# The order of an encoder kernel's engines, found on a simulated timeline instead of the plain model

## The chip, the core and the metric

The kernel runs on one core of one Trainium2 chip. The metric is the device time of one execution in microseconds (us). A core has five engines that each work through their own list of instructions in order and wait for one another by semaphores: PE (TensorE, matmuls; its weight loads are shown apart as PEld), DVE (VectorE), ACT (ScalarE), POOL (GpSimd) and SP (SyncE, which here only issues DMAs). A profile is one execution taken by the hardware profiler.

## The reference

A two-layer encoder over 512 tokens of width 1024. Each layer projects the normalised input, runs five mixers side by side on parts of the projection, gates their outputs with gates computed from the input, sums them, and closes with an output matmul and a layer norm:

```python
h = layer_norm(x, ln_in_g, ln_in_b)
for l in range(DEPTH):
    p = jnp.einsum('bsd,dc->bsc', h, w_in[l])
    pa, pb, pc, pd, pm = split_last(p, mixer_sizes)
    o_a = mixer_dilated(pa, table_a)
    o_b = mixer_rwkv(pb, ...)
    o_c = mixer_axial_gqa(pc, ...)
    o_d = mixer_diff(pd, ...)
    o_m = mixer_memory(pm, mem, w_mem_kv[l])
    y = gated_merge(h, (o_a, o_b, o_c, o_d, o_m), w_branch[l], w_gate[l], b_gate[l])
    out = jnp.einsum('bsd,de->bse', y, w_out[l])
    h = layer_norm(alpha * h + out, ln_g[l], ln_b[l])
```

Four mixers are attentions over 512 or 256 keys (A dilated, C grouped-query, D differential, M memory). The fifth, B, is a recurrence over the tokens in both directions, eight heads. `gated_merge` is, per mixer, `sigmoid(h @ w_gate) * (o @ w_branch)`.

## The kernel before, in words

**The work.** All activations stay on the core; weights stream in from DRAM in blocks of 128x512 (`load_w`, L125, issued by SP into two buffers per channel, `wrawr` and `wrawf`). A matmul at nearly full fp32 precision is made of three fast ones: `split_w` turns each weight block into a high part (ACT, L135) and a low part (DVE, L136), and `gemm3_steps` issues high x high, high x low and low x high (L149, L150, L151), each 128x512.

**The stages of a layer.** Attention comes first (`att`): for A, C, D and M in turn it projects q, k, v (PSUM tile `pg`), scores (`psc`, L444), softmax on DVE and ACT, transposes (`pt`, L470) and multiplies by v (`po`, L479, L489). For A, D and M `k_stack` copies k to the other half of the partitions by POOL's DMAs (L435, L437). Then the recurrence (`rw`): eight units, one for each pair of heads and direction. `early` prepares a unit (L812 to L941, with the score-like matmuls at L881), `late` solves it: 31 dependent steps of two DVE instructions (L963 and L965), the block inversion on PE (L981, L988), then L1009, L1024, L1035, and a chain of eight states in which PE (L1042), ACT (L1044) and DVE (L1045) take turns. `finish` (L1066 to L1091) normalises a pair of heads. Last comes the out stage: the merge of branch B, the output matmul, the layer norm.

**The filler.** The merge of the other four branches is traced as a generator, `fill`, that is pulled a few matmuls at a time between the steps of C, of M and of the recurrence, and drained after it. Its matmuls go to one PSUM tile of their own, `pf`, so that PE has something to do where the stages have not; in this text they are called filler. There are 1104 of them in a layer, always 128x512: for each of four branches and eight output blocks, 24 for the gate and 6 or 12 for the branch. To each such block belong two or three weight blocks with their splits, an ACT tanh (L380) and two DVE instructions (L388, L390). Branch outputs but A's are spilled to DRAM (`scr_o`) and read back by POOL's DMAs (L366) when four tiles `o` are free.

```python
for _ in recurrence():
    pull(1)
for _ in fl:
    pass
```

**What sets the order.** The kernel's code does not fix an order across the stages. It is traced under the framework's tile context, and every instruction gets its rank from the place where it is traced. When the context closes, a scheduler plays the program against a model of the machine: whenever an engine is free in the model, it gets the instruction of the best rank whose inputs and buffers are ready there. The lists that come out are fixed, one for each engine, and the chip works through them as they stand. So a filler matmul that is traced within the recurrence moves ahead into attention wherever the model shows PE idle there.

## Time and profile before

| | |
|---|---|
| median of 3 runs | 2260.18 us (2258.39 to 2260.19) |
| profiled execution, its own time | 2261.37 us |
| its span | 2259.6 us |
| PE busy | 2186.5 us, 97% |
| DVE busy | 1730.6 us, 77% |
| ACT busy | 1273.2 us, 56% |
| POOL busy | 59.6 us, 3% |
| mean granted TensorE clock | 0.999 of full speed |

Busy time is the union of an engine's instructions. The ends of matmuls are modelled and matmuls overlap, so a PE that shows as busy need not run at its peak. Around the span lie 1.8 us of the execution's own time.

### The profile page before, as it was taken

How to read it: one execution, taken by the hardware profiler on the slowest of the kernel's cores; microseconds unless marked ns; L12 is line 12 of the kernel's file. 1: busy time of each engine (PE TensorE's matmuls, PEld its weight loads, DVE VectorE, ACT ScalarE, POOL GpSimd, SP SyncE). 2: the span in 40 equal slices, each digit the busy share in tenths (PEclk: the TensorE clock that was granted, in tenths of full speed). 3: DMA queues.
4: the chain of work that ended last, by engine and by line, in shares of the span. 5: the costliest groups of instructions: out<-in, count | busy, mean ns of one | idle time of the engine just before them, and what ended most of it. 6: DMA issues, size and time to landing. Idle time of an engine off the chain costs nothing.

```text
span 2259.6 us, 36239 instructions
## 1 busy us (share of the span) xinstructions
PE 2186.5 (97%) x13056; PEld 1678.6 (74%) x13056; DVE 1730.6 (77%) x4236; ACT 1273.2 (56%) x2785; POOL 59.6 (3%) x117
## 2 busy tenths in 40 slices
PE   6999999999999999999999999999999999999998
PEld 5777777777767777777787777777777777777776
DVE  7677887677989797975568778766788979879565
ACT  3565666676665555644326656677675646565440
POOL 0000000100000000000000000001000000000000
PEclk9999999999999999999999999999999999999999
DMA  7732124322222221315333312333313213222261
GB/s 261 222 108 91 56 80 112 113 86 85 75 80 66 86 88 59 102 49 181 117 115 108 98 62 70 97 106 89 112 57 99 71 62 98 72 80 73 84 195 38
DMA packets 111780, 220.49 MB, mean 98 GB/s; under 512 B 13240, under 2 KB 23224, under 8 KB 111216
## 3 DMA queue, kind: packets, MB, share of 16 engines
q1 hardware_dynamic: 101456, 195.09, 27.0%
q0 software_dynamic: 10144, 23.08, 4.0%
q8 instruction: 103, 1.69, 0.3%
q14 instruction: 77, 0.63, 0.1%
HBM read 187.66 MB, written 27.31 MB: 95 GB/s over the span
## 4 chain that ended last, share of the span: by engine, by line
PE 70%; DVE 14%; ACT 8%; DMA 5%; issue 3%; DVEq 0%; POOL 0%; ACTq 0%; SPq 0%
PE pg L150 10%; PE pg L151 10%; PE pg L149 10%; PE pf L149 6%; PE pf L150 5%; PE pf L151 5%; PE psc L444 4%; PE po L489 3%; PE pt L470 3%; DVE W L965 2%; DVE pr L963 2%; DMA wrawr<-in_w_out_dram 1%; DVE wlof L136 1%; PE po L479 1%; DMA wrawf<-in_w_mem_dram 1%
## 5 line engine op out<-in xcount | busy, mean ns | idle before, releaser
L149 PE MATMUL pg<-hT,whir 128*128 128x512 f32 (+1 forms) x912 | 364.0, 399 | 3.2 <-DVE kl L436 1.4
L150 PE MATMUL pg<-hT,whir 128*128 128x512 f32 (+1 forms) x912 | 365.4, 401 | 0.5 <-DVE hT L176 0.5
L151 PE MATMUL pg<-hT,wlor 128*128 128x512 f32 (+1 forms) x912 | 363.8, 399 | 2.1 <-DVE wlor L136 2.1
L136 DVE TENSOR_TENSOR wlor<-wrawr,whir 128x512 fp32r<-128x512 f32 x240 | 163.9, 688 | 114.8 <-ACT whir L135 104.9
L135 ACT CAST whir<-wrawr 128x512 fp32r<-128x512 f32 x240 | 147.7, 618 | 175.1 <-PE pg L150 116.7
L135 ACT CAST whif<-wrawf 128x512 fp32r<-128x512 f32 (+1 forms) x272 | 164.4, 605 | 135.4 <-PE pf L150 77.9
L149 PE MATMUL pf<-hT,whif 128*128 128x512 f32 x512 | 220.8, 431 | 3.4 <-DVE gt L388 2.8
L136 DVE TENSOR_TENSOR wlof<-wrawf,whif 128x512 fp32r<-128x512 f32 (+1 forms) x272 | 181.4, 669 | 49.2 <-ACT whif L135 43.2
L150 PE MATMUL pf<-hT,whif 128*128 128x512 f32 x512 | 206.7, 404 | 0.0
L151 PE MATMUL pf<-hT,wlof 128*128 128x512 f32 x512 | 205.2, 401 | 0.0
L149 PEld LDWEIGHTS pg<-hT,whir 128*128 128x128 f32 x912 | 172.0, 189 | 40.6 <-issue 3.0
L151 PEld LDWEIGHTS pg<-hT,wlor 128*128 128x128 f32 x912 | 171.9, 188 | 40.0 <-DVE wlor L136 4.9
L150 PEld LDWEIGHTS pg<-hT,whir 128*128 128x128 f32 x912 | 171.9, 189 | 37.8 <-issue 3.9
L176 DVE TENSOR_TENSOR pT<-pt,pT 128x512 fp32r<-128x512 f32 x176 | 114.2, 686 | 34.2 <-ACT pT L175 33.1
L175 ACT CAST pT<-pt 128x512 fp32r<-128x512 f32 x176 | 94.7, 589 | 63.0 <-PE pt L470 61.7
L149 PEld LDWEIGHTS pf<-hT,whif 128*128 128x128 f32 x512 | 96.5, 188 | 35.8 <-DVE gt L388 10.2
L470 PE MATMUL pt<-cst,p 128*128 128x128 f32 x704 | 118.6, 273 | 0.5 <-DVE p L461 0.5
L151 PEld LDWEIGHTS pf<-hT,wlof 128*128 128x128 f32 x512 | 96.4, 188 | 22.2 <-issue 1.6
L963 DVE TENSOR_TENSOR pr<-W,U 128x60 f32<-128x60 f32 (+24 forms) x496 | 103.5, 209 | 11.4
L965 DVE TENSOR_TENSOR W<-W,pr 128x60 f32<-128x60 f32 (+24 forms) x496 | 102.9, 208 | 11.0
L470 PEld LDWEIGHTS pt<-cst,p 128*128 128x128 f32 x704 | 89.8, 141 | 28.4 <-DVE p L461 3.6
L150 PEld LDWEIGHTS pf<-hT,whif 128*128 128x128 f32 x512 | 96.8, 189 | 18.8 <-issue 4.3
(326 smaller groups left out, 4809.1 us busy)
## 6 DMA issues: line engine op xcount, KB each, us to landing
wrawr<-in_w_in_dram SPq DMA_DIRECT2D x224, 256.0 KB, 2.8
wrawf<-in_w_gate_dram SPq DMA_DIRECT2D x160, 256.0 KB, 2.8
o<-scr_o POOLq DMA_DIRECT2D x26, 512.0 KB, 4.5
wrawf<-in_w_branch_dram SPq DMA_DIRECT2D x48, 256.0 KB, 2.7
bias<-scr_toe SPq DMA_DIRECT2D x24, 448.0 KB, 3.3
scr_o<-os SPq DMA_DIRECT2D x20, 512.0 KB, 3.7
wrawf<-in_w_in_dram SPq DMA_DIRECT2D x32, 256.0 KB, 3.0
wrawr<-in_w_out_dram SPq DMA_DIRECT2D x32, 256.0 KB, 2.9
```

What stands on the lines that cost most here:

```text
L135: nc.scalar.copy(hi, raw)
L136: tt(lo, raw, f(hi), ALU.subtract)
L149: mm(ps, ah, bh, start=(i == 0), stop=False)
L150: mm(ps, ah, bl, start=False, stop=False)
L151: mm(ps, al, bh, start=False, stop=(i == n - 1))
L175: nc.scalar.copy(hi, src)
L176: tt(lo, src, f(hi), ALU.subtract)
L444: mm(ps[:, :nk], q[:, i, sl], part[:, i if g is None else g, :nk], start=(j == 0), stop=(j == 1))
L470: nc.tensor.transpose(pt[:, qb * 128:(qb + 1) * 128], p4[qb][:, kb * 128:(kb + 1) * 128], ident)
L489: mm(po, vwin(kb), pT[:, b, :], start=(kb == 0 and b == 0), stop=(kb == nkb - 1 and b == 1))
L963: tt(pr, W[:, t8, s:s + 1].to_broadcast([128, nt, n]), U[:, s:s + 1, rsl].to_broadcast([128, nt, n]), ALU.mult)
L965: tt(W[:, t8, rsl], W[:, t8, rsl], pr, ALU.add)
```

## The change

One keyword. The scheduler's machine model is no longer the plain one but the framework's timeline simulation; ranks, buffers and every instruction stay as they were. All five lists are found anew.

```diff
     o = nc.dram_tensor("out_0_dram", (S, DM), F32, kind="ExternalOutput").ap()
-    with tile.TileContext(nc) as tc:
+    with tile.TileContext(nc, schedule_with_timeline_sim=True) as tc:
         encoder_kernel(tc, *[args[k] for k in _INS], o)
```

What that does to the lists is shown at three places of the first layer; the second layer has the same pattern. In the rows, `pf` is a filler matmul, `pg` a projection, `psc<-kh` and `psc<-kc` a score.

PE in attention C, second block of heads, at the third score of its second half. Before:

```order
L149 MATMUL pg<-hT,whir 128x512
L444 MATMUL psc<-kh,q 128x512
L444 MATMUL psc<-kc,q 128x512
L150 MATMUL pg<-hT,whir 128x512
L444 MATMUL psc<-kh,q 128x512
L444 MATMUL psc<-kc,q 128x512
L151 MATMUL pg<-hT,wlor 128x512
```

The same score now:

```order
L149 MATMUL pf<-o,whif 128x512
L444 MATMUL psc<-kh,q 128x512
L444 MATMUL psc<-kc,q 128x512
L150 MATMUL pf<-o,whif 128x512
L151 MATMUL pf<-o,wlof 128x512
L470 MATMUL pt<-cst,p 128x128 x2
L149 MATMUL pf<-o,whif 128x512
L150 MATMUL pf<-o,whif 128x512
L151 MATMUL pf<-o,wlof 128x512
```

Between two scores that had one projection matmul between them there now stand eleven filler matmuls (the next six continue the pattern) and two transposes.

PE in the recurrence, in the chain of states (L1042) of a unit past its middle. Before:

```order
L1042 MATMUL pt<-ST_5175,PE 128x128
L149 MATMUL pf<-o,whif 128x512
L150 MATMUL pf<-o,whif 128x512
L151 MATMUL pf<-o,wlof 128x512
L940 MATMUL psc<-kes,cst 128x512
L149 MATMUL pf<-o,whif 128x512
L150 MATMUL pf<-o,whif 128x512
L151 MATMUL pf<-o,wlof 128x512
L1042 MATMUL pt<-ST_5176,PE 128x128
```

The chain of such a unit now:

```order
L1042 MATMUL pt<-ST_5175,PE 128x128
L1024 MATMUL pt<-OM,WA 64x128 x4
L1042 MATMUL pt<-ST_5176,PE 128x128
L1042 MATMUL pt<-ST_5175,PE 128x128
L1024 MATMUL pt<-OM,WA 64x128 x4
L1035 MATMUL pt<-UV,OM 64x64 x16
L1042 MATMUL pt<-ST_5176,PE 128x128
L881 MATMUL psc<-AR,BK 128x128 x8
L1042 MATMUL pt<-ST_5175,PE 128x128
```

No filler is left between the states; what stands there is the recurrence's own small matmuls.

Counted in PE's lists of the first layer, up to the first L981 (the first solved unit), from there to the last unit's first L981, and behind it: of 1104 filler matmuls 261, 753 and 90 stand there before, and 944, 160 and none now. The 160 come in the first two of the seven intervals between units; five have none. In the second layer the three counts are the same. Other matmuls of 128x512 move too: 54 projections (`pg`) of the first layer now come ahead of its first L981. From the first layer's last unit to the second layer's first, 351 filler matmuls, 1628 `pg` and 519 `psc` stood in the list, and now 944, 1680 and 478; behind the second layer's last unit, 90 filler matmuls and 192 `psc` stood, and now none and 144.

POOL from attention D's first head to its second (a piece of the difference; `kh` and `kl` are the copies of k, `o` a branch output that the filler reads):

```order
 L435 DMA kh<-kh 64x512
 L437 DMA kl<-kl 64x512
+L366 DMA o<-scr_o 128x1024 x2
+L435 DMA kh<-kh 64x512
+L437 DMA kl<-kl 64x512
+L435 DMA kh<-kh 64x512
+L366 DMA o<-scr_o 128x1024
+L437 DMA kl<-kl 64x512
+L366 DMA o<-scr_o 128x1024
 L435 DMA kh<-kh 64x512
 L437 DMA kl<-kl 64x512
```

The read-back of branch C's outputs, which came behind all of attention in POOL's list, now stands among the copies of k for D's heads.

In SP's list all twelve `scr_toe` writes (L270, tables of the position bias) now stand ahead of the ninth weight block (`wrawr` and `wrawf`, L125); before, the first four stood behind the eleventh block and the others between later ones.

## Rows read from the trace of the kernel before

**Rows 1.** The page, engines and slices: busy us, and the granted clock in tenths.

```profile
PE 2186.5 (97%) x13056; PEld 1678.6 (74%) x13056; DVE 1730.6 (77%) x4236; ACT 1273.2 (56%) x2785; POOL 59.6 (3%) x117
PEclk9999999999999999999999999999999999999999
```

**Rows 2.** The page, the chain that ended last, its shares of the span by engine.

```profile
PE 70%; DVE 14%; ACT 8%; DMA 5%; issue 3%; DVEq 0%; POOL 0%; ACTq 0%; SPq 0%
```

**Rows 3.** Five stretches: start:end, length, busy us (x instructions), clock, DMA share, GB/s.

```profile
0.00:610.30 610.30, 581.42 (x2898) 455.52 (x2899) 464.91 (x1064) 371.00 (x774) 23.86 (x48) 1.00 0.38 118
610.30:1000.40 390.10, 378.52 (x2940) 281.42 (x2941) 331.65 (x928) 224.25 (x543) 5.94 (x11) 1.00 0.25 77
1000.40:1708.50 708.10, 698.51 (x3483) 543.82 (x3483) 516.16 (x1155) 404.14 (x833) 22.82 (x45) 1.00 0.32 100
1708.50:2098.50 390.00, 378.46 (x2939) 281.42 (x2939) 331.61 (x928) 224.25 (x543) 5.94 (x11) 1.00 0.25 77
2098.50:2259.60 161.10, 149.57 (x798) 116.38 (x798) 86.26 (x165) 49.52 (x92) 1.08 (x2) 0.98 0.33 108
```

**Rows 4.** The same view, filler alone (tile pf): PE, PEld, DVE, ACT.

```profile
610.30:1000.40 390.10, 216.05 (x753) 132.19 (x753) 14.48 (x22) 15.04 (x22) 1.00 0.25 77
```

**Rows 5.** PE's timeline, a run of projections: start, length; the first and the fifteenth.

```profile
540.08 0.39 PE L150 MATMUL pg<-hT,whir 128*128 128x512 f32 x1
...
543.33 0.39 PE L149 MATMUL pg<-hT,whir 128*128 128x512 f32 x1
```

**Rows 6.** Stretches again: most of attention A to D, and two of the out stage.

```profile
100.00:550.00 450.00, 445.48 (x2117) 346.53 (x2116) 339.37 (x772) 289.50 (x592) 17.59 (x35) 1.00 0.31 95
...
2150.00:2200.00 50.00, 49.04 (x208) 38.43 (x207) 32.45 (x51) 25.55 (x45) 0.00 (x0) 1.00 0.61 194
2200.00:2250.00 50.00, 50.00 (x218) 40.62 (x217) 23.61 (x51) 1.51 (x3) 0.00 (x0) 1.00 0.09 32
```

**Rows 7.** Groups from 610.3 to 1000.4, the filler's DVE instructions: busy, mean ns, idle before.

```profile
L136 DVE TENSOR_TENSOR wlof<-wrawf,whif 128x512 fp32r<-128x512 f32 x60 | 40.9, 684 | 0.8 <-ACT whif L135 0.7
L388 DVE SCALAR_TENSOR_TENSOR gt<-gt,pf 128x512 f32<-128x512 f32 x21 | 14.3, 683 | 1.9 <-PE pf L151 1.6
L390 DVE TENSOR_TENSOR y<-y,gt 128x512 f32<-128x512 f32 x20 | 13.7, 687 | 0.2
```

**Rows 8.** Waits from 610.3 to 1000.4: us in total, times, longest.

```profile
ACT UV L1003 <- PE pt L1035: 19.1, 6, 3.6
ACT ST L1044 <- PE pt L1042: 14.3, 17, 1.6
DVE nkk L783 <- ACT tmp L205: 10.3, 3, 4.6
```

**Rows 9.** The page, DMA issues: KB each, median us from issue to landing.

```profile
o<-scr_o POOLq DMA_DIRECT2D x26, 512.0 KB, 4.5
```

**Rows 10.** Stretches again: the one in which the first tables are written.

```profile
46.00:54.00 8.00, 5.77 (x34) 4.76 (x33) 1.66 (x3) 2.65 (x6) 0.00 (x0) 1.00 1.07 387
```

**Rows 11.** The chain behind the second layer's last unit: start, us; finish's first matmul.

```profile
2125.41 1.07 PE po L1066 x30
```

**Rows 12.** Stretches at the end, where PE has run out of work.

```profile
2250.00:2254.00 4.00, 0.70 (x4) 0.23 (x2) 3.16 (x8) 0.00 (x0) 0.00 (x0) 0.98 0.00 0
2254.00:2257.00 3.00, 0.00 (x0) 0.00 (x0) 2.41 (x9) 0.00 (x0) 0.00 (x0) 0.50 0.05 18
```

## The prediction

> **What bounds the kernel now.** I read the page first, then the chain of waits, then stretches cut where a layer's recurrence solves its first unit and its last (the first L981 of each). The page has PE busy for 97% of the span, at full clock throughout [rows 1], and the chain that ended last runs through PE for 70% of it, through DVE for 14% [rows 2]. Per stretch, with A up to the first layer's first unit, B its recurrence, C from there to the second layer's first unit, D that recurrence, E the rest: A shows PE busy for 581 of 610 us, C for 699 of 708, and DVE for 465 and 516. In B and D PE is busy for 378 of 390 us and DVE for 332 [rows 3]. Of PE's 378 the 753 filler matmuls cover 216 [rows 4]. So the recurrence by itself does not need PE much; DVE is its engine, and the filler is what keeps PE full beside it. Attention needs PE all the time.
>
> How much room is left inside "busy" is read from the spacing of starts. Fifteen 128x512 matmuls in a row start 3.25 us apart from first to last, 0.232 us each, while each shows 0.39 us [rows 5]. A stretch that shows PE busy for 49.04 of 50 us holds 208 matmuls, the next one, at 50.00, holds 218 of the same kind [rows 6]. So even a stretch that shows as full can have some 5% of room, and not much more.
>
> **The change.** The lists show that it moves PE's work from where PE was cover to where PE is the bound. The plain count: 683 filler matmuls more ahead of the first unit (944 against 261), 593 fewer in each recurrence (160 against 753), 593 more in C (944 against 351), 90 fewer in E. I price each at 0.232 us.
>
> *Stretch A.* 683 x 0.232 = 158 us, and the 54 projection matmuls that came along 12.5 us, together 171 us of PE work more. What PE's idle time takes of it: in 100 to 550 us PE shows 4.5 us idle [rows 6], the lower end, and 5% of these 450 us is 22 us, the upper. I take 10 off, between them, since the filler goes in exactly where the new model saw PE waiting, but PE's list can't step aside where the chip waits elsewhere. At the start SP's list has eight of the twelve table writes moved ahead of weights. 512 KB each, 4.2 MB, take 11 us at the 387 GB/s of the stretch that writes the first four [rows 10]; nothing is the lower end, because what is written early needn't be written later, when PE waits for weights as well. I take 5. A: 171 - 10 + 5 = +166 us.
>
> *Stretch C.* 593 x 0.232 = 138 us, 52 projections more 12 us, 41 gate matmuls (`psc`) fewer -9.5 us: +140. Room as in A, 10 us; against it, the last unit of the first layer has lost 90 filler matmuls that ran beside its chain, 21 us, of which I let 6 come back as idle PE. C: 140 - 10 + 6 = +136 us.
>
> *Stretches B and D.* They lose the filler's share. On PE that is 593 x 0.232 = 138 us, on DVE less: the filler's splits, sums and products there take 40.9 + 14.3 + 13.7 = 69 us for 753 matmuls [rows 7], so 593 take 54 us with them. What ends the recurrence is DVE and the exchange between engines, not PE's throughput: DVE is busy for 332 us of 390, idle for 58, and its waits are for ACT and PE in the solving chain (L1003 for L1035 19.1 us, L1044 for L1042 14.3 us, L783 for ACT 10.3 us) [rows 8], which stays as it is. One end: DVE without its idle time, 332 - 54 = 278 us, 112 less than now. The other: no gain, if the chain's latency fills the time. I take DVE's saving with its idle time unchanged: PE answers the chain faster with no filler queued ahead, but DVE has fewer independent instructions between two waits. B and D: -54 us each.
>
> *Stretch E.* 90 filler and 48 gate matmuls fewer, 32 us of PE work. But from the last unit's first L981 (2098.5) to finish's first matmul pass 27 us [rows 11], in which PE's filler was cover and not cause. The 48 gate matmuls, 11 us, do come off, the 90 (21 us) only in part. I take -17, ends -32 and -11.
>
> *The rest.* POOL's read-backs now stand ahead of copies of k that attention D waits for, and wait themselves for the last filler of branch A. In PE's list that filler ends ahead of the second D head's scores in the new order too, so the wait is over when PE gets there; if not, two read-backs of 4.5 us to landing [rows 9] delay one head, 9 us a layer at most. I take nothing. Every instruction is still there, so nothing else is gained.
>
> **Sum**, against the profiled execution's 2261.4 us (the median of the runs is 2260.2, 1.2 less): +166 + 136 - 54 - 54 - 17 = +177, 2438 us. That is 8% slower. Its own range is 2370 to 2505: the room in A and C from 4.5 to 22 us each, the start from 0 to 11, E's ends, and B and D by 25 us each around -54.
>
> **Rivals.**
>
> *The recurrence falls to DVE's time.* Without filler ahead of it in PE's list every answer to DVE comes at once, and DVE's idle time nearly vanishes. For it: the new DVE list weaves the 31 steps of one unit through the states of the unit before. Against it: the idle time is spent on ACT as much as on PE. B and D -105 each, A and C with 22 us of room, E -32: 2261 + 154 + 124 - 210 - 32 = 2297 us.
>
> *The clock falls.* Where PE runs dry, the trace shows what happens: in the 3 us from 2254, after PE's last matmul at 2250, the granted clock is 0.50, the 1.2 GHz level [rows 12]. Five of seven intervals between units have no filler now. PE's other work there is 378 - 216 = 162 us [rows 3, 4] and the 160 filler matmuls that stay 37; twice the 200 us is more than the 336 that I forecast, PE is the bound again, and B and D give nothing back: 2261 + 166 + 136 - 17 = 2546 us. Against it: PE's list still has small matmuls at every step of the chain there. The Trainium skill, page "TensorE: Matmul & The Clock Gate", the closing table "Why this matters for your kernels", speaks against this change: it warns of idle gaps between bursts of matmuls, after which the clock is back at half. By that rule the time is the 2546 us. The trace agrees at the kernel's end alone; the slices before it all show the full clock [rows 1].
>
> *The filler is free in attention.* The one that ends faster. If PE in attention spends a good part of its "busy" time waiting, filler costs nothing there, while the recurrence still gets shorter. PE's weight loads are busy for 999 of the 1318 us of A and C [rows 3], which leaves 24%, 319 us, and the work added is 311. Then only the start and the gains are left: 2261 + 5 - 108 - 17 = 2141 us. It turns to the fast side once A and C absorb some 197 of the 311 us. Against it: the stretch that is full of nothing but 128x512 matmuls shows weight loads at 40.62 of 50 us, 81%, and attention 346.5 of 450, 77% [rows 6], so 81% is full and the room is 5% again. The Trainium skill, page "Perfetto Trace Analysis", section "Identifying the Most-Contended Engine", says that matmul busy time is a poor measure and to judge headroom by the busy share of LDWEIGHTS; read as it stands, with 100% as full, that gives the 2141 us. The trace agrees that matmul busy time hides waits, but not with 100%.
>
> *Nothing comes of it.* The lists do differ at the places where PE is short of time, so an unchanged time needs gains and losses that cancel.
>
> **How the numbers follow.** A difference of 0.2%, 4.5 us, is about what a measurement of this kernel can tell from no change. Forecast 0.64; DVE's floor 0.16; the clock 0.13; free filler 0.05; no difference 0.02. The first three are slower by far over 0.2%: faster 0.05, same 0.02, slower 0.93. The range goes from 2290, which takes in most of the DVE case, to 2530, short of the full clock case: left out are the two small cases, part of the clock's and a little of DVE's.
>
> **What would show it.** In the profile after: A lengthened by some 166 us and C by some 136, with PE busy as now; between the first and the last L981 of a layer some 336 us with DVE at 275 to 280 us busy and PE near half; the filler's last matmul in the third unit. Wrong in size, if that stretch is nearer 285 or 390 us. Wrong in kind, if A and C grow by less than 100 us each.

## The result, and the profile after

The changed kernel takes 2569.84 us (median of 4 runs, 2567.25 to 2571.63), beside 2259.28 us for the kernel before on the same chip: ratio 1.1371, 95% interval 1.1358 to 1.1385. It is slower by 310 us; the forecast was +177 and its range ended at 2530 us. The side was right, the size was not.

The page of the kernel after, engines, granted clock in 40 slices, and the shares of the chain that ended last ([rows 1, 2] before):

```profile
PE 2295.4 (89%) x13056; PEld 1828.0 (71%) x13056; DVE 1766.3 (69%) x4236; ACT 1271.1 (50%) x2779; POOL 61.0 (2%) x117
PEclk9999999999999977776999999999999998675689
PE 71%; DVE 16%; ACT 6%; DMA 4%; issue 3%; SPq 0%; DVEq 0%; ACTq 0%
```

PE, DVE and POOL have as many instructions as before; ACT has six fewer, all of them table loads (2779 against 2785 in [rows 1]). PE's busy time grew by 109 us, but the span by 306: PE waits more than before. And the clock, which showed full throughout, has two valleys.

The same five stretches, cut at the first and the last unit's first L981 of each layer (start:end, length, then PE, PEld, DVE, ACT, POOL busy, clock, DMA share, GB/s); they answer to [rows 3]:

```profile
0.00:809.40 809.40, 754.38 (x3643) 607.39 (x3644) 541.98 (x1171) 427.00 (x865) 29.98 (x58) 0.99 0.37 116
809.40:1165.20 355.80, 283.19 (x2335) 221.57 (x2334) 284.34 (x843) 177.16 (x466) 1.62 (x3) 0.78 0.12 37
1165.20:2058.80 893.60, 848.11 (x4089) 679.10 (x4089) 582.84 (x1240) 451.81 (x908) 27.79 (x53) 0.97 0.32 98
2058.80:2409.80 351.00, 280.73 (x2335) 220.52 (x2335) 283.89 (x843) 174.31 (x464) 1.61 (x3) 0.78 0.12 37
2409.80:2565.20 155.40, 128.96 (x658) 99.39 (x658) 73.29 (x143) 40.77 (x76) 0.00 (x0) 0.85 0.24 83
```

A is 199 us longer (forecast 166), C 185.5 (136). B and D give back 34 and 39 (54 each), E 6 (17). Look at PE's idle time, length less busy: 29 us before and 55 now in A, 10 and 45 in C, 12 and 73 in B. I had expected A and C to use up idle time; they made more of it.

The filler alone (tile pf) in the first two stretches: 944 matmuls ahead of the first unit, and the rest beside the first units, as the lists said (161 and not 160 here, since one lies across the cut).

```profile
0.00:809.40 809.40, 247.57 (x944) 176.15 (x944) 17.80 (x26) 17.80 (x26) 0.99 0.37 116
809.40:1165.20 355.80, 43.26 (x161) 30.17 (x160) 4.10 (x6) 4.11 (x6) 0.78 0.12 37
```

PE's longest waits over the whole span (us in total, times, longest):

```profile
PE pt L981 <- DVE U L977: 48.0, 7, 14.1
PE pt L1042 <- DVE ST L1045: 32.1, 31, 3.6
PE pf L149 <- DVE gt L388: 29.0, 18, 3.6
PE pg L149 <- DVE k L740: 20.4, 2, 10.4
```

Three of the four are the recurrence's: PE waits for a unit to be solved, for a state, for a prepared k. The third is the filler itself, which in a dense row waits for its one PSUM tile. None of this explains why A and C grew by 82 us more than forecast. So the question for the runs is whether the filler's place did it, or the rest of the new order.

### The profile page after: what moved, and what is told of

Read it like the earlier page. It is cut to its first block, busy times and chain, and to the rows that moved or that the text cites. A ratio compares the mean times of both kernels' runs of the same rounds, so it can differ in the third digit from the quotient of the medians.

```text
span 2565.2 us, 36429 instructions
## 1 busy us (share of the span) xinstructions
PE 2295.4 (89%) x13056; PEld 1828.0 (71%) x13056; DVE 1766.3 (69%) x4236; ACT 1271.1 (50%) x2779; POOL 61.0 (2%) x117
## 4 chain that ended last, share of the span: by engine, by line
PE 71%; DVE 16%; ACT 6%; DMA 4%; issue 3%; SPq 0%; DVEq 0%; ACTq 0%
PE pg L149 10%; PE pg L150 10%; PE pg L151 10%; PE pf L149 6%; PE pf L150 6%; PE pf L151 6%; PE psc L444 3%; PE pt L470 3%; PE po L489 3%; DVE pr L963 1%; DVE W L965 1%; PE psc L881 1%; PE pt L1042 1%; DMA wrawr<-in_w_out_dram 1%; PE pt L1035 1%
## 5 line engine op out<-in xcount | busy, mean ns | idle before, releaser
L135 ACT CAST whir<-wrawr 128x512 fp32r<-128x512 f32 x240 | 148.3, 618 | 222.4 <-PE pg L150 158.2
L149 PE MATMUL pf<-hT,whif 128*128 128x512 f32 x512 | 211.3, 413 | 29.2 <-DVE gt L388 29.0
L149 PEld LDWEIGHTS pg<-hT,whir 128*128 128x128 f32 x912 | 177.1, 194 | 70.2 <-issue 26.4
L150 PE MATMUL pf<-hT,whif 128*128 128x512 f32 x512 | 206.0, 402 | 0.0
L150 PEld LDWEIGHTS pg<-hT,whir 128*128 128x128 f32 x912 | 176.9, 194 | 37.9 <-DVE hT L176 0.9
L458 ACT ACTIVATE p<-p,sst 128x512 f32<-128x512 f32 x128 | 92.4, 722 | 51.3 <-DVE sst L452 50.7
L470 PE MATMUL pt<-cst,p 128*128 128x128 f32 x704 | 110.4, 273 | 0.5 <-DVE p L461 0.5
```

Source lines behind the costliest of these rows:

```text
L135: nc.scalar.copy(hi, raw)
L149: mm(ps, ah, bh, start=(i == 0), stop=False)
L150: mm(ps, ah, bl, start=False, stop=False)
L458: act(p, src, AF.Exp, scale=-1.0, bias=st[:, 0:1], accum_out=st[:, 1:2])
L470: nc.tensor.transpose(pt[:, qb * 128:(qb + 1) * 128], p4[qb][:, kb * 128:(kb + 1) * 128], ident)
```

## The experiments

Theory 1: the filler's place is all. Theory 2: the rest of the new order, which I had priced at nothing, costs as much again. A third possibility was that it gains.

### The filler's place and the rest, apart

**hold**: the timeline order, with the filler queued on PE behind the matmul traced just ahead of it.

```diff
-        owed = [0.0]
+        owed, main, seen = [0.0], [], [len(nc.cur_bb.bb.instructions)]
 
         def pull(x):
             owed[0] += x
+            main.extend(i for i in nc.cur_bb.bb.instructions[seen[0]:] if i.engine == mybir.EngineType.PE)
             while owed[0] >= 1:
                 owed[0] -= 1
-                next(fl, None)
+                with tc.issue_after(main[-1 - 0]):
+                    next(fl, None)
+            seen[0] = len(nc.cur_bb.bb.instructions)
```

> The changed kernel (the simulated timeline finds the order), with every filler matmul queued on PE behind the matmul that is traced just ahead of it: 180 filler matmuls ahead of the first unit's first L981, 834 between, 90 behind (before: 261, 753, 90; the change: 944, 160, 0). All else is free to move. Theory 1, the place of the filler alone makes the change slower: within 1.2% of the kernel before, 2235 to 2287 us, the recurrence near 390 us. Theory 2, the rest of the new order (attention's own order, the early table writes, the recurrence's weave) costs as much again as the filler: 2340 us or more. Theory 3, the rest of the new order gains and the filler's place costs more than it shows: under 2230 us.

Measured: 2438.26 us, ratio 1.0803 (1.0779 to 1.0827). With the filler back beside the recurrence 180 us are still lost: theory 2.

**early**: the plain order, with the filler pulled early.

```diff
-                        pull(0.7)
+                        pull(2.95)
...
                         p4.append(p0)
+                        pull(4.5)
...
-                        pull(0.3)
+                        pull(3.7)
...
-            for _ in recurrence():
-                pull(1)
+            for j, _ in enumerate(recurrence()):
+                pull(4 if j < 19 else 0.17)
```

> The kernel before, its scheduler unchanged, with the pulls of the filler made earlier: 2.95 steps per block of attention C, 4.5 per block of D, 3.7 of M, 4 at each of the recurrence's first 19 yields, 0.17 behind them. Filler ahead of the first L981 918, between first and last 186, behind 0; attention C's last score has 273 ahead of it, D's 483, M's 648 (the change: 310, 501, 672). Theory 1 (place alone): 2520 to 2590 us, attention stretches as long as in the change. Theory 2 (the rest of the order costs as well): 2400 to 2470 us, about what I forecast for the move itself. Theory 3: over 2590 us.

Measured: 2416.61 us, ratio 1.0695 (1.0677 to 1.0713), +158 us; again theory 2. Its five stretches:

```profile
0.00:753.90 753.90, 728.92 (x3499) 571.46 (x3499) 525.41 (x1146) 411.52 (x841) 29.21 (x58) 1.00 0.38 120
753.90:1089.40 335.50, 294.11 (x2479) 215.27 (x2479) 286.73 (x868) 195.03 (x493) 1.61 (x3) 0.92 0.14 47
1089.40:1935.80 846.40, 825.82 (x3946) 644.00 (x3947) 563.59 (x1215) 435.42 (x884) 27.21 (x53) 0.97 0.32 100
1935.80:2269.20 333.40, 290.20 (x2477) 211.53 (x2477) 286.65 (x868) 194.77 (x493) 1.61 (x3) 0.93 0.15 48
2269.20:2419.90 150.70, 127.49 (x658) 99.52 (x658) 73.44 (x143) 40.80 (x76) 0.00 (x0) 0.85 0.25 86
```

This is nearly the move that the forecast worked out, 918 filler matmuls ahead of the first unit where the change has 944, and the plain model orders the rest. Against [rows 3] A is +143.6 us for 657 filler matmuls more ahead of the first unit, 0.219 each; C +138.3 for 567 (918 against 351), 0.244 each; B and D are -54.6 and -56.6, with DVE at 287 us busy. Attention took none of the moved filler for nothing: in the second layer C's scores, from first to last, take 140.4 us in place of 93.5 with 189 filler matmuls more among them, and D's 149.5 in place of 112.5 with 180 more.

**bare** and **bare_timeline**: no filler, in the plain order and in the timeline order.

```diff
-        fl = fill()
+        fl = iter(())
...
-                if y[db] is None:
+                if y[db] is None and done is None:
...
-                        tt(gt, y[db], gt, ALU.add)
```

> The kernel before without the filler: the gates and merges of the branches A, C, D and M are left out, so the sum over branches holds B alone. From the stretches: 2261 less filler's place on PE in A (60 us), C (81), E (21) and with some 340 us in each recurrence: about 2000 us. By my price for room in attention (5%) the stretches A and C lose 55 and 75 us. If the filler was free there (rival), A stays at 605 us. The recurrence: 336 us if DVE's work with its idle time sets it; near 350 or more with a granted clock under 0.8 if the lower clock lengthens it; 280 us if DVE alone.

> The changed kernel without the filler (the same work left out). Theory 1 (place alone): within 1.5% of the same cut made from the kernel before. Theory 2 (the rest of the order costs): 60 us or more above it, in the attention stretches. Theory 3: 30 us or more below it.

Measured: 2088.99 us (ratio to the kernel before 0.9251, 0.9235 to 0.9267) and 2255.89 us (0.9990, 0.9979 to 1.0001). The rest of the new order costs 167 us where there is no filler at all. The stretches of bare, then of bare_timeline:

```profile
0.00:598.10 598.10, 543.05 (x2677) 422.27 (x2677) 451.33 (x1042) 361.81 (x756) 23.83 (x48) 0.97 0.35 113
598.10:926.00 327.90, 259.46 (x2196) 190.78 (x2197) 261.31 (x820) 172.32 (x450) 1.63 (x3) 0.79 0.09 30
926.00:1612.10 686.10, 635.99 (x3124) 490.66 (x3125) 485.16 (x1103) 386.19 (x799) 21.74 (x43) 0.95 0.28 90
1612.10:1935.60 323.50, 253.47 (x2195) 186.90 (x2196) 261.10 (x820) 172.18 (x450) 1.63 (x3) 0.81 0.09 30
1935.60:2087.80 152.20, 128.94 (x658) 100.61 (x658) 68.38 (x135) 40.99 (x76) 0.00 (x0) 0.85 0.26 85
```

```profile
0.00:669.20 669.20, 562.20 (x2695) 442.24 (x2695) 458.84 (x1045) 363.35 (x757) 23.75 (x48) 0.93 0.32 101
669.20:1010.00 340.80, 258.70 (x2181) 202.78 (x2181) 268.71 (x816) 167.24 (x446) 1.64 (x3) 0.71 0.09 28
1010.00:1761.50 751.50, 653.33 (x3140) 511.70 (x3140) 494.70 (x1106) 388.32 (x800) 21.92 (x43) 0.92 0.26 82
1761.50:2100.90 339.40, 248.75 (x2181) 194.13 (x2181) 268.42 (x816) 167.22 (x446) 1.63 (x3) 0.75 0.09 28
2100.90:2253.70 152.80, 127.90 (x658) 99.97 (x658) 68.30 (x135) 40.75 (x76) 0.00 (x0) 0.85 0.25 85
```

Nearly the same work in each stretch, and A is 71 us longer, B 13, C 65, D 16, E 1. In hold, which has its filler at about the place of the kernel before (180 matmuls ahead of the first unit, 261 there), the rest can be read a second time. Its A and C, against [rows 3]:

```profile
0.00:685.90 685.90, 597.40 (x2876) 472.08 (x2878) 472.75 (x1065) 376.81 (x778) 23.60 (x48) 0.95 0.32 104
...
1088.50:1865.60 777.10, 711.43 (x3459) 558.94 (x3459) 525.98 (x1155) 409.85 (x836) 22.78 (x45) 0.96 0.28 90
```

Side by side, from the profiled executions:

| | filler's place (early - before) | rest (bare_timeline - bare) | sum | rest again (hold - before) | measured (after - before) | forecast |
|---|---|---|---|---|---|---|
| A | +143.6 | +71.1 | +214.7 | +75.6 | +199.1 | +166 |
| B | -54.6 | +12.9 | -41.7 | +12.5 | -34.3 | -54 |
| C | +138.3 | +65.4 | +203.7 | +69.0 | +185.5 | +136 |
| D | -56.6 | +15.9 | -40.7 | +10.4 | -39.0 | -54 |
| E | -10.4 | +0.6 | -9.8 | +7.1 | -5.7 | -17 |
| all | +160.3 | +165.9 | +326.2 | +174.6 | +305.6 | +177 |

The two measures of the rest agree within 7 us in every stretch, and the filler's place and the rest nearly add up. A and C stay 16 and 18 us under their sums, as if the filler took up some of the idle time that the rest of the order makes there; B is 7 over.

What was expected of bare alone did not come: about 2000 us, with A and C shorter than before by 55 and 75 us. Without their 261 and 351 filler matmuls they are only 12.2 and 22.0 us shorter. So the filler that stood there before cost 0.05 and 0.06 us each, against 0.22 and 0.24 for what early moved in. It had found time that PE had over: 150 of the 261 stand between attention's last score and the first unit, where bare shows PE idle for 22.8 of 104.2 us, and with them this piece takes 100.2 us and leaves 2.7 idle. One caution: leaving work out also finds all lists anew. D's scores, for one, take 123.9 us in bare and 112.5 in the kernel before.

### What in the rest of the order costs

In the second layer, bare against bare_timeline: attention A's scores span 106.1 and 115.5 us, C's 95.3 and 108.4, D's 123.9 and 146.2, and the recurrence 323.5 and 339.4. The scores of A, C and D are 45 of the 65 us by which the stretch C grew. C and D from first to last score, bare:

```profile
1244.70:1340.00 95.30, 92.06 (x448) 69.39 (x448) 86.19 (x197) 61.89 (x134) 2.07 (x4) 1.00 0.21 67
1340.80:1464.70 123.90, 119.23 (x523) 90.33 (x524) 87.48 (x209) 83.22 (x161) 8.15 (x16) 0.99 0.33 99
```

and bare_timeline:

```profile
1351.00:1459.40 108.40, 99.33 (x474) 76.39 (x473) 88.49 (x194) 63.70 (x134) 2.21 (x4) 1.00 0.22 68
1461.70:1607.90 146.20, 130.21 (x556) 99.27 (x555) 95.12 (x223) 88.38 (x170) 7.66 (x15) 0.95 0.29 88
```

In C DVE is busy for 86 of 95 us, almost as full as PE; my view of attention as PE's alone left that out. The new order puts 26 and 33 matmuls more into C and D, and PE, DVE and ACT all idle more there. In D, bare, three of the waits:

```profile
DVE kl L435 <- ACT kh L433: 13.8, 3, 4.7
DVE wlor L136 <- ACT whir L135: 6.8, 7, 2.0
...
ACT whir L135 <- PE pg L150: 5.4, 4, 1.9
```

and bare_timeline:

```profile
DVE wlor L136 <- ACT whir L135: 20.9, 13, 4.3
...
ACT whir L135 <- PE pg L150: 17.8, 9, 4.8
```

DVE's longest wait in bare, for the copies of k, is not among those of bare_timeline; there it waits for the weight blocks. ACT's copy of a weight block waits for the projection matmul that frees its buffer, DVE's split waits for that copy, and the softmax instructions behind the split in DVE's list wait with it. In PE's lists 96, 142 and 96 projection matmuls more stand ahead of the second, third and fourth head's first score of D. That gave theory J: the projections taken early are the cover that attention lacks later.

**hold_proj**, **bare_hold_proj**: hold and bare_timeline, with attention's projections held as well.

```diff
     def proj(ps, l, blk, hT, ch="r"):
         w = split_w(w_in[l, blk], 1024, ch)
-        gemm3(ps, [(*wk(w, k), hT[:, 0, k, :], hT[:, 1, k, :]) for k in range(8)])
+        pe = [i for i in nc.cur_bb.bb.instructions[-1400:] if i.engine == mybir.EngineType.PE]
+        with ExitStack() if 16 <= blk < 34 else tc.issue_after(pe[-1 - 24]):
+            gemm3(ps, [(*wk(w, k), hT[:, 0, k, :], hT[:, 1, k, :]) for k in range(8)])
```

> The held kernel (timeline order, filler queued at its traced place, 2438 us), in which attention's projections are held too: each is queued on PE behind the 25th matmul traced ahead of it. Projection matmuls ahead of attention D's second, third and fourth head's first score are then 840, 936, 1032 in layer 0 (before: 840, 936, 1032; held: 924, 1056, 1128). Theory J, the projections taken early are the cover that attention lacks later, as the filler is the recurrence's: 2280 to 2330 us; what is left is the start (10 us) and the recurrence's weave (some 12 us a layer). Theory V, DVE's and ACT's order sets attention's time: 2390 us or more.

> The changed kernel without the filler (2256 us) with attention's projections held in the same way. Theory J: attention C and D go from 108.5 and 146 us back to within 4 us of the plain order's 95.4 and 124, the whole to 2120 to 2160 us. Theory V: C and D stay over 104 and 140 us, the whole over 2215 us.

**bare_jump**: the plain order, with the next head's projections traced ahead of a head's scores (`prep` holds the lines that make k, q and v).

```diff
+                nxt = prep(0)
                 for h in range(4):
...
+                    k, q, v = nxt
+                    if h < 3:
+                        nxt = prep(h + 1)
                     b = load_bias(8 + h)
```

> The kernel before without the filler (2089 us), plain scheduler, with the projections of k, q and v of attention D's next head traced ahead of the scores of the head before: 38, 36 and 24 projection matmuls more ahead of the second, third and fourth head's first score (the timeline order: 96, 142, 96 more). Theory J: a part of the 22 us by which D is longer under the timeline order, 3 to 12 us a layer, 2094 to 2115 us in all. Theory V: within 3 us of 2089.

Measured: 2572.57, 2384.66 and 2092.20 us. Theory J falls as a way back: held projections make both kernels some 130 us slower still. D alone:

```profile
1565.90:1701.70 135.80, 116.74 (x459) 83.04 (x457) 77.02 (x188) 77.89 (x148) 8.14 (x16) 0.92 0.29 82
1534.00:1565.90 31.90, 30.44 (x138) 23.76 (x137) 19.82 (x35) 14.88 (x28) 2.04 (x4) 1.00 0.38 103
```

It goes from 146.2 to 135.8 us, but between C's last score and D's first there now stand 31.9 us of projections where 2.3 stood. C, at 109.9, gains nothing. The 24 to 38 projections that bare_jump takes early make D's scores 3 us longer (127.0), but M's 3 us shorter, and 2092.20 us lies 3 us over bare, within the spread of the runs (2086.36 to 2094.73): it says little either way. That the projections taken early cost D time is so neither shown nor refuted; taking them back by force does not pay.

**bare_pe**, **bare_dve_act**, **bare_queues**: the plain order, with some engines' lists pinned to the timeline order's. **bare_tl_plain_pe**, **bare_tl_plain_da**: the reverse. The engines not named are ordered around the pinned lists. `ORDER` (left out here) holds the places of an engine's instructions in the list that is wanted, packed as text; `skip` names branches, semaphores and the like.

```diff
+def pin(tc, nc):
...
+    for eng, code in ORDER.items():
+        ins = [i for i in nc.cur_bb.bb.instructions if i.engine == eng and i.opcode not in skip]
+        ks = np.cumsum(np.frombuffer(zlib.decompress(base64.b85decode(code)), "<i2")) - 1
...
+        for a, b in zip(ks, ks[1:]):
+            tc.add_manual_dep(ins[b], ins[a].name, mybir.DependencyInfo(
+                mybir.DependencyClass.NoSync, mybir.DependencyReason.DATA), reason="pin")
...
         encoder_kernel(tc, *[args[k] for k in _INS], o)
+        pin(tc, nc)
```

> The kernel before without the filler (2089 us), plain scheduler, with PE's list alone pinned to the list that the timeline scheduler gave for the same cut (2256 us); the other engines' lists are found around it. Theory P, PE's list is what the rest of the new order costs (it puts a matmul where the model saw its operand ready, and PE waits in line where the chip is later): 2220 to 2270 us. Theory V, it is the order on DVE and ACT: under 2150 us. Theory Q, it is the order of the transfers: under 2150 us.

> The same cut of the kernel before (2089 us), with the lists of DVE and ACT pinned to the timeline scheduler's, PE's and the queues' found around them. Theory V: 2220 us or more. Theory P: 2090 to 2170 us, as far as PE's list has to follow.

> The same cut of the kernel before (2089 us), with the lists of SP and POOL, which issue the transfers, pinned to the timeline scheduler's. Theory Q: 2200 us or more. Theories P and V: 2085 to 2110 us, of which the first scores' delay by the early table writes is 5 to 11 us (my forecast took 5).

> The changed kernel without the filler (2256 us; plain order 2089), timeline scheduler, with PE's list alone pinned to the plain order's; DVE, ACT and the queues are ordered around it by the simulated timeline. Theory P, PE's list alone carries the cost: under 2130 us. Theory V, DVE's and ACT's lists carry it: 2220 us or more. Theory M, lists made apart wait for one another whichever is kept (as in the two pinned runs before, 2397 and 2405): over 2256 us.

> The same cut of the changed kernel (2256 us), with the lists of DVE and ACT pinned to the plain order's, PE and the queues ordered around them by the simulated timeline. Theory V: under 2140 us. Theory P: 2220 us or more. Theory M: over 2256 us.

Measured, between 2089 us in the plain order and 2256 in the timeline order:

| | pinned to the timeline order, rest plain | pinned to the plain order, rest timeline |
|---|---|---|
| PE | 2397.08 | 2215.00 |
| DVE and ACT | 2405.34 | 2447.53 |
| SP and POOL | 2116.08 | - |

Three of the four mixtures of PE's list with DVE's and ACT's are slower than both parents, as theory M has it: lists made apart wait for one another. The waiting itself was not traced, and no run pins a kernel to its own lists, so what the pinning alone costs is not known. The question which engine's list is to blame has therefore no simple answer, and neither theory P nor theory V holds alone. bare_tl_plain_pe says where PE's list matters. Its C and D:

```profile
1340.00:1426.00 86.00, 78.03 (x366) 58.36 (x365) 77.26 (x169) 53.42 (x115) 2.04 (x4) 0.97 0.21 69
1426.00:1551.10 125.10, 119.01 (x525) 89.54 (x524) 85.57 (x204) 82.66 (x160) 8.16 (x16) 0.99 0.31 94
```

With the plain order's list on PE, D is 125.1 us, 1.2 from bare, with 525 matmuls in place of 556. The timeline's list on PE and the others found around it (bare_pe) make it 159.5 us. So D's 22 us go with PE's list. C (the first row has its second part) takes 102.2 from first to last score, half way back from 108.4 to 95.3. But its recurrences, 334.9 and 336.9 us, have only 6 and 2.5 us less than bare_timeline's, and its A is 49 us longer than bare's: these go with the lists that the timeline made for the other engines. The queues' list costs 27 us: A is 33.6 longer and C 15.5, while both recurrences got shorter, by 13.0 and 7.9. Its first three stretches:

```profile
0.00:631.70 631.70, 552.69 (x2683) 428.32 (x2683) 449.50 (x1042) 362.20 (x757) 23.18 (x48) 0.95 0.34 107
631.70:946.60 314.90, 247.75 (x2191) 180.54 (x2192) 261.44 (x820) 171.40 (x448) 1.63 (x3) 0.83 0.09 31
946.60:1648.20 701.60, 643.42 (x3128) 496.26 (x3128) 485.63 (x1103) 386.25 (x800) 21.73 (x43) 0.94 0.28 88
```

**bare_tl_ring**, **bare_ring**, **ring**: three buffers for the split weights, in both orders without the filler and in the complete kernel. One buffer of the spilled tile `os` makes the room.

```diff
-            hi = wp.tile([128, 512], F32R, name="whi" + ch, tag="whi" + ch, bufs=2)[:, :w]
-            lo = wp.tile([128, 512], F32R, name="wlo" + ch, tag="wlo" + ch, bufs=2)[:, :w]
+            hi = wp.tile([128, 512], F32R, name="whi" + ch, tag="whi" + ch, bufs=3 if ch == "r" else 2)[:, :w]
+            lo = wp.tile([128, 512], F32R, name="wlo" + ch, tag="wlo" + ch, bufs=3 if ch == "r" else 2)[:, :w]
...
-            t = pool.tile([128, 2, S], F32R, name="os", tag="os", bufs=2) if out else new_o()
+            t = pool.tile([128, 2, S], F32R, name="os", tag="os", bufs=1) if out else new_o()
```

> The same cut of the changed kernel (2256 us), with three buffers in place of two for the split weights of the projections (whir, wlor; for their room the spilled tile os has one in place of two). In attention D of this cut DVE's splits wait 20.9 us a layer for ACT's copies and these 17.8 us for the projection matmuls that release a buffer; with the plain order it is 6.8 and 5.4. Theory W, this ring is what ties the three lists together: attention D from 146 to under 136 us and the whole under 2200 us, and the plain order gains less than 20 us from the same buffers. Else: within 25 us of 2256 us.

> The kernel before without the filler (2089 us), plain order, with the same three buffers for the split weights. Theory W: 2065 to 2090 us. Else: within 10 us of 2089 us.

> The kernel before (2259 us), complete and in the plain order, with three buffers in place of two for the split weights of the projections (whir, wlor; os has one in place of two for the room). Without the filler the same buffers gave 24 us. With the filler PE is the bound (97% busy), and the buffers remove waits of ACT and DVE rather than work of PE: 2240 to 2262 us. If they gain as much as without the filler: 2235 us.

Measured: 2280.73, 2065.26 and 2259.49 us (the last 1.0010, 1.0000 to 1.0019). Theory W falls: in the timeline order the buffers make it 25 us slower, D 148.3 us. In the plain order they gain 24 us without the filler and nothing with it, where PE is at 97% either way. No complete version found here beats the kernel before.

### The clock

**warm**: bare, with matmuls that nobody reads among the recurrence's own.

```diff
+            idr = rp.tile([128, 128], F32R, name="idr", tag="idr", bufs=1)
+            nc.scalar.copy(idr, ident)
+            seen = len(nc.cur_bb.bb.instructions)
             for _ in recurrence():
-                pull(1)
+                main = [i for i in nc.cur_bb.bb.instructions[seen:] if i.engine == mybir.EngineType.PE]
+                if main:
+                    with tc.issue_after(main[-1]):
+                        ps = ps_f()
+                        for _ in range(2):
+                            mm(ps, idr, hT[:, 0, 0, :], start=True, stop=True)
+                seen = len(nc.cur_bb.bb.instructions)
```

> The same cut of the kernel before (2089 us), with 382 matmuls of 128x512 that nobody reads put behind the recurrence's own (two behind each of its steps that has matmuls, 162 x 2 of them between a layer's first and last L981, 75 us of PE at 0.232 us). They keep PE busy without work for DVE. Without them the recurrence takes 327.9 and 323.5 us at a granted clock of 0.79 and 0.81. If the lower clock lengthens the recurrence, it gets shorter with them, at a clock of 0.9 or more: under 318 us. If DVE and the exchange set it whatever the clock: 322 to 335 us. If the added work itself is in the way: over 335 us.

Measured: 2062.93 us, 26 less than bare with 764 matmuls more, 382 in each layer. The second, the fourth and the last stretch:

```profile
596.40:912.20 315.80, 298.42 (x2515) 214.40 (x2515) 264.19 (x818) 171.37 (x449) 1.63 (x3) 0.97 0.09 30
...
1598.70:1915.70 317.00, 299.46 (x2516) 215.13 (x2517) 264.27 (x819) 171.38 (x449) 1.64 (x3) 0.96 0.09 30
1915.70:2062.10 146.40, 128.18 (x700) 99.05 (x700) 69.41 (x137) 41.66 (x77) 0.00 (x0) 0.96 0.27 92
```

The clock goes from 0.79 and 0.81 to 0.97 and 0.96, the recurrences from 327.9 and 323.5 to 315.8 and 317.0, the last stretch from 152.2 to 146.4. In the last stretch nearly the same lists ran (133 of DVE's 134 instructions stand in bare's order), so its 5.8 us go with the clock, 0.85 against 0.96.

In the recurrence two things changed at once. DVE's list was found anew: at most 511 of its 819 instructions there stand in bare's order, as few as in bare_timeline (508). And bare_queues, at a clock of 0.83 and 0.82, has recurrences as short as warm's, 314.9 and 315.6 us, with another list (709 of 819). So the 12.1 and 6.5 us that warm takes off the recurrences can be the clock, the list or both; that the lower clock lengthens the recurrence is not shown.

## Why the prediction was wrong, step by step

**The step that failed is "The rest".** It took nothing for all that moves besides the filler and the few projections that it counted. The runs put this at +166 us in the profiled executions without the filler (71 in A, 65 in C, 13 and 16 in B and D) and at +180 us with the filler held. It is as large as the filler's own move, and without it the range would have held the time: early, at 2416.61 us, lies in the likeliest case's own range. The argument "every instruction is still there, so nothing else is gained" looked at gains alone. Five lists found anew can also lose everywhere.

*A and C.* The price of 0.232 us a filler matmul stood: 0.219 and 0.244 in early. "Some 5% of room, and not much more" stood as well: early's A is 9 us under 657 x 0.232 = 152 us, about the 10 us taken off, and its C 7 us over 567 x 0.232 = 132. The mistake was to let the new order use that room. I argued that filler goes in where the model saw PE waiting; the profile after shows 55 and 45 us of idle PE where 29 and 10 stood.

*The start.* 5 us forecast for the early table writes. With the queues' list alone the first score comes 4.9 us later (59.0 against 54.1 us), in the change itself 9.7 us (63.8). But with the queues' list alone the stretch grows by 33.6 us, and 22.8 of these lie in attention A's scores (156.3 us from first to last against 133.5): the transfers' order behind the first score, which I did not price. In bare_timeline A's scores take 144.1 us, so the price differs with the other lists.

*B and D.* -54 each for the filler's share of DVE, with DVE's idle time unchanged: early has -54.6 and -56.6, that is 335.5 and 333.4 us where 336 was forecast. That this came out so closely was in part luck: in B DVE's busy time fell by 45 us and its idle time by 10 (58.4 to 48.8), for 567 filler matmuls fewer, where the forecast had 54 and nothing for 593. In the change, with 355.8 and 351.0 us, 13 and 16 us go with the rest of the new order, which the prediction left out here ("which stays as it is"). DVE is busy for 284 us, close to the 275 to 280 of the forecast. "PE near half" was wrong: PE shows 283 of 355.8 us, and without any filler 259 of 327.9 in bare, where the forecast had 162 left by taking the filler's 216 from 378.

*E.* -17 forecast, -10.4 in early and -5.7 in the change: the 90 filler matmuls ran for almost nothing there. Early is at the lower end that I named, -11, and the change past it.

*POOL's read-backs.* Not tried apart. bare_timeline reads nothing back for the filler and loses 71 and 65 us in A and C all the same, so they are not what the rest costs.

*The range.* The ends that the prediction names for it add up to 2344 and 2511 us, not 2370 and 2505; the profiled execution's 2567 lies outside either.

**The rivals.** *The recurrence falls to DVE's time*: no, DVE idles for 71 of 355.8 us. *The clock falls*: its 2546 us are the nearest number, but not its reason. The clock did fall, to 0.78 in B and D, and yet B and D gave back 34 and 39 us; PE shows 73 us idle in B and is not its bound. The Trainium skill's warning (page "TensorE: Matmul & The Clock Gate", table "Why this matters for your kernels") that idle gaps cost clock agrees with the trace: 0.78 where PE idles for 73 of 355.8 us. What it is worth is 5.8 us in warm's last stretch; for a recurrence warm's 12.1 and 6.5 us do not settle it, since the list changed as well. *The filler is free in attention*: no, not what the change moved there. The weight loads show 607 of 809 us in A, 75%, and early paid 0.219 and 0.244 us for each matmul moved. What the kernel before already had there was nearly free, and with it the free time was used up. The Trainium skill's measure, the busy share of the weight loads (page "Perfetto Trace Analysis", section "Identifying the Most-Contended Engine"), does not agree with this trace when it is read with 100% as full. *Nothing comes of it*: no.

**What stays open.** That the whole of the new order costs 166 us is shown, and where; that D's 22 us of it go with PE's list is shown. Why its recurrence and its first stretch are slower is not traced to a single cause, and how much of it the lower clock (0.71 and 0.75 in bare_timeline's recurrences, 0.79 and 0.81 in bare's) adds is open. Holding projections and a larger weight ring did not give the time back. The waits of DVE for ACT and of ACT for PE in D are seen, but that they are the cause was only argued.

## What to carry to other kernels

A scheduler option that finds all lists anew is no local edit: price the loss of fit between engines as well as the moves that can be counted, and take out the largest move first (early and hold are one edit each) to see what is left. Filler is cheap as far as its engine has idle time beside it, and is paid in full beyond that: the 2208 matmuls cost 172 us in the kernel before (2259.6 against 2087.8), 0.078 each; the 753 in a recurrence cost 62.2 and 66.5 us, 0.08 to 0.09 each; and those that were moved ahead of it, into stretches whose room was used, 0.22 to 0.24 each. Lists from two schedules can be worse than either: three of four mixtures here were, by 141 to 192 us against the slower parent.

## What the runs showed of the hardware that was not expected

More PE work made a kernel faster: 764 matmuls that nobody reads took 26 us off 2089, at a granted clock of 0.97 in place of 0.79 in the first recurrence; 5.8 of these 26 us, in the last stretch, came with nearly the same lists. In the clock's valley of the kernel after, two rows show it, a 50 us stretch and the projections in it:

```profile
950.00:1000.00 50.00, 34.31 (x254) 27.34 (x252) 40.81 (x135) 21.44 (x62) 0.00 (x0) 0.64 0.05 17
...
L149 PE MATMUL pg<-hT,whir 128*128 128x512 f32 x8 | 4.5, 557 | 10.4 <-DVE k L740 10.4
```

The clock of 0.64 lies between the two levels of 1.2 and 2.4 GHz, nearer the lower. A 128x512 projection matmul shows 557 ns there, where [rows 5] have 390 at full clock, after PE had waited 10.4 us for a vector instruction. And pinning the queues' list alone, which left DVE's busy time in the recurrence as it was (261 us), shortened the recurrences from 327.9 and 323.5 to 314.9 and 315.6 us; why is open.
